# Sums of weight tiles in the SwiGLU pairs: from GpSimd to VectorE, with two low parts formed by ScalarE and an accumulating DMA, and the DRAM sums of the last weights issued earlier

## The chip, the cores and the metric

The kernel runs on one core of one Trainium2 chip. The metric is the time of one execution on the device in microseconds (us). The kernel before the change took 811.02 us (median of three runs: 810.82, 811.02 and 812.86).

Five engines work side by side, and the text uses the profile's names for them: PE multiplies matrices (PEld is its loading of weights), DVE (VectorE) and POOL (GpSimd) work on whole tiles, ACT (ScalarE) does activations and casts, and SP (SyncE) only issues transfers here. Each runs its own list of instructions in order and waits on semaphores for the others. Transfers (DMA) are issued by SP or by POOL and carried out by 16 DMA engines.

## What is computed

One decoder block on x of shape 512 x 1024 in float32, cut to what matters:

```python
h = rmsnorm(x, norm1_g)
z_glu, z_rx, z_rg, z_ga, z_gb = split(h @ w_in + b_in)   # the input stage
y_a = convolution mixer of z_glu, then @ conv_w_out + conv_b_out
y_b = (linear recurrence of z_rx, times gelu(z_rg)) @ lru_w_out
x = x + (sigmoid(z_ga) * y_a + sigmoid(z_gb) * y_b) @ w_mix_out
h = rmsnorm(x, norm2_g)
x = x + (silu(h @ ffn_w1) * (h @ ffn_w3)) @ ffn_w2       # SwiGLU, D_FF = 2816
return rmsnorm(x, norm_f_g)
```

## The kernel before, in words

**Products.** A product in float32 is made of three faster ones: each operand is kept as a high part (its value rounded) and a low part (what the rounding left), and PE multiplies high by high, high by low and low by high. Every weight tile is loaded by SP into a raw buffer of 128 x 1024 (512 KB; tag `raw`, 8 buffers). ACT casts it to the high part (`split_to`, line 124), and DVE or POOL subtracts high from raw to make the low part (`sub`, line 120; the argument `lo` says which engine). Both parts lie in one buffer of tag `hl` (5 of them). The tiles stand in one list, `chunks`. `weights(key)` asks for a tile and brings everything up to four tiles further (`AHEAD`) into the program at the same place; `emit_chunk` writes the load, the cast and the subtraction of one tile, and calls what the list has under `after`.

**Stages.** The input stage goes through a table of 60 tokens (`ORDER`); each makes one or two tiles of z (24 matmuls a tile) or, in tokens `h`, gates of the recurrence. POOL makes the low parts of nearly all its weights. Then come eight steps with the weights of the recurrence's output (tiles `lo`), eight steps with those of the convolution's output (`co`), the product with `w_mix_out`, the SwiGLU, and the products with `ffn_w2` (line 1247, results `or`). In the first stages the order of PE, ACT, DVE and SP is the one written in the code; in the SwiGLU loop the framework's scheduler places the instructions of each engine, and keeps their dependencies.

**The SwiGLU pairs.** D_FF is taken in 11 pairs of 2 x 128 columns. Pair 0 is plain. Each of the pairs 1 to 10 multiplies the 2 x 2 blocks of h and of the weights by a scheme of seven products in place of eight (class `Seven`). The seven weight tiles of a pair are b11, b21, b22, t2, t1, t3 and t4; w1 and w3 lie side by side in the halves of a tile, and each product takes 24 matmuls of 256 columns (line 1441). t1 to t4 are sums and differences of b11, b12, b21 and b22. For pairs 1 to 3 they are made in the input stage by POOL and stored in DRAM (`make_f_sums`). For pairs 4 to 10 `f_fly(k)` makes them where they are used: SP loads the four tiles (line 382, two transfers of 256 KB each, one for w1 and one for w3), and POOL makes four sums in the raw buffers themselves (`in_line`): b12 + b22 goes over b12 and is t3, that plus b11 goes over b11 and is t2, b22 minus t2 goes over b22 and is t1, b21 plus t2 goes over b21 and is t4. All seven low parts of such a pair are made by DVE.

Beside these, DVE adds and subtracts the results out of PSUM (`c11`, `q`, `c12`, `c21`), ACT applies SiLU to one half of each (`out_of`, line 1458), and DVE multiplies the halves (line 1459, into `ou` and `ov`).

**The sums of the last weights.** The products with `ffn_w2` use the same scheme, and its sums t1 to t4 (tiles `ot1` to `ot4` in DRAM) are made by transfers alone: `out_sums` is a generator of 48 transfers from DRAM to DRAM, 24 plain copies (line 486) and 24 that add to what is there (line 487), nearly all of 512 KB, interleaved over six groups. POOL issues them. In the kernel before, `in_line` draws from this generator between POOL's sums (1, 3 and 3 in each pair); each is placed behind the newest sum.

Of the kernel before, what the change touches and what calls it, by code (L numbers as in the profile page):

```python
# [8 lines left out]
F32 = mybir.dt.float32  # L9
F32R = mybir.dt.float32r  # L10
AF = mybir.ActivationFunctionType
ALU = mybir.AluOpType

P = 128
# [38 lines left out]
BEGUN, BEGUN_LATER = (1, 2), (3,)  # L53
STORED = BEGUN + BEGUN_LATER
OUT_SUMS_OF = 2
SUMS_AT, SUMS_STEP, SUMS_LAG, STORE_LAG = 3, 5, 2, 2
STORED_LAG = 3
SUMS_OWN = 40
# [26 lines left out]
def tile_block(ctx, tc, a, out):  # L85
# [24 lines left out]
    vec, act, pe, pool_e = nc.vector, nc.scalar, nc.tensor, nc.gpsimd  # L110


    add = lambda o, x, y: vec.tensor_tensor(out=o, in0=x, in1=y, op=ALU.add)  # L113
    plus_on = lambda eng, o, x, y: eng.tensor_tensor(out=o, in0=x, in1=y, op=ALU.add)  # L114

    newest = {}
    put_off = []

    def sub(eng, o, x, y):
        return eng.tensor_tensor(out=o, in0=x, in1=y, op=ALU.subtract)  # L120

    def split_to(h, l, full, eng, copy=act.copy):

        copy(h, full)  # L124
        if eng is None:
            put_off.append((l, full, h.bitcast(F32)))
            return h, l
        last = sub(eng, l, full, h.bitcast(F32))
        newest["sub" if eng is pool_e else "low"] = last.ins
        return h, l  # L130
# [26 lines left out]
    def wchunk(key, src, kt, cols, where="hl", lo=pool_e, after=None):  # L157
        chunks.append((key, src, kt, cols, where, lo, after))
# [191 lines left out]
    def f_quarter(n, k, w_, c0, c1):  # L350

        c, j = 4 * (int(n[1]) - 1), 2 * k + int(n[2]) - 1
        return w_[:, c + c0 : c + c1, j * P : (j + 1) * P]
# [20 lines left out]
    def f_fly(k):  # L374

        q = {}

        def new(n):
            q[n] = raw_t = raws.tile([P, 1024], F32, tag="raw", name=f"raw_f{n}_{k}")
            for i, w_ in enumerate((w1, w3)):  # L380
                src = f_quarter(n, k, w_, 0, 4)
                newest["any"] = nc.sync.dma_start(raw_t[:, i * T : (i + 1) * T].rearrange("p (k n) -> p k n", k=4), src).ins
            return raw_t

        def in_line(n, make, *what):
            with tc.issue_after(newest["sum"]) if "sum" in newest else nullcontext():
                newest["sum"] = make(pool_e, *what).ins
            for _ in range(n):
                next(out_steps, None)

        def first():
            raw_t = new("b11")
            new("b12")
            return raw_t

        def sums_32():
            in_line(0, plus_on, q["b12"], q["b22"], q["b12"])
            in_line(1, plus_on, q["b11"], q["b12"], q["b11"])

        def sums_14():  # L400
            in_line(3, sub, q["b22"], q["b11"], q["b22"])
            in_line(3, plus_on, q["b21"], q["b21"], q["b11"])

        for n, load, after in (
            ("b11", first, None), ("b21", lambda: new("b21"), None), ("b22", lambda: new("b22"), sums_32),
            ("t2", lambda: q["b11"], sums_14), ("t1", lambda: q["b22"], None), ("t3", lambda: q["b12"], None), ("t4", lambda: q["b21"], None),
        ):
            wchunk(f"f{n}_{k}", None, 8, P, where=load, lo=vec, after=after)

    def f_chunks(k, some=("b2", "t0", "t1")):  # L410

# [78 lines left out]
    def out_sums():  # L490

        rows = outq.w.rearrange("p (k i) n -> p i k n", i=2)
        jobs = []
        for k0 in range(0, KF, OUT_SUMS_OF):
            ks = slice(k0, min(k0 + OUT_SUMS_OF, KF))
            jobs.append(dram_sums(lambda i, h: rows[:, i, ks, h * T : (h + 1) * T], {n: v[:, ks, :] for n, v in outq.all_sums.items()}))
        for start, dst, src in (one for of in zip(*jobs) for one in of):
            with tc.issue_after(newest["sum"]):
                start(dst, src)
            yield  # L500

# [441 lines left out]
    def run_beside(n):  # L943
        for _ in range(n):
            if not beside_one():
                break
            room[0] -= 1
# [203 lines left out]
    f_todo = [f_piece(k, i, c) for k in STORED for i in range(2) for c in range(2)]  # L1151
    f_sums_steps = make_f_sums()
    out_steps = out_sums()
    with tc.manual_schedule(engines={ET.PE, ET.Activation, ET.DVE, ET.SP}):
        for kind, j in ORDER:
            next(f_sums_steps, None)
            if kind == "u" and j < EARLY:
                for _ in glu(j, in_mm(GLU + j), in_mm(GLU + 8 + j)):
                    pass
                run_beside(2)  # L1160
                emit_to(emitted[0] + 2)
                continue
            if kind == "u":
                pv = step(GLU, j)
                end_step()
                later(glu(j, pv, step(GLU + 8, j)), 1)
            elif kind == "rx":
                later(rx(j, step(RX, j)), 1)
            elif kind == "rg":
                later(rg(j, step(RG, j)), 1)  # L1170
            elif kind == "gb":
                later(half_sig(j, step(GB, j)), 1)
            elif kind == "ga":
                later(sig(GA, j, step(GA, j), sga, "sga"), 1)
            elif kind == "h":
                later(heads(j, head_mms(j)))
                continue
            end_step()
        while held_back:
            at_step[0] += 1  # L1180
            run_due()


    for j in range(8):
        ws = w_tiles(f"lo{j}_0", 5) + w_tiles(f"lo{j}_1", 5)
        ps = bank(f"yb{j}")
        mm3(ps, ws, y)
        vec.scalar_tensor_tensor(out=sgb[j], in0=sgb[j], scalar=1.0, in1=ps, op0=ALU.add, op1=ALU.mult)
        run_beside(7)
        next(f_sums_steps, None)  # L1190
        if j in (2, 4, 6):
            mixq.make_sums(j // 2 - 1)
    yb = sgb
# [116 lines left out]
    for n, j in enumerate(mixq.order()):  # L1310
        ws = w_tiles(f"co{j}", ND)
        ps = bank(f"ya{j}")
        mm3(ps, ws, un)
        o = sga[j]
        vec.scalar_tensor_tensor(out=o, in0=ps, scalar=pc("conv_b_out", j), in1=o, op0=ALU.add, op1=ALU.mult)
        m7.tile(j, lambda cs, dst: add(dst, o[:, cs], yb[j][:, cs]))
        if n == 0:
            mixq.make_sums(3)
        if n == 5:
            x2 = [[longt(f"x2{t}{h}") for h in range(2)] for t in range(NT)]  # L1320
            for t in range(NT):
                for h in range(2):
                    nc.sync.dma_start(x2[t][h], x_nat[:, t, h * T : (h + 1) * T])
        next(f_sums_steps, None)

    for _ in f_sums_steps:
        pass


# [131 lines left out]
    class Seven:  # L1461
# [14 lines left out]
        def copy(self):  # L1476
            self.c11 = shortt(f"c11_{self.k}")
            left_over(act.copy(self.c11, self.r1).ins)
# [242 lines left out]
```

## Time and profile before

| | us |
|---|---|
| median of three runs | 811.02 |
| the profiled execution | 811.09 |
| its span, first to last instruction | 809.3 |
| PE busy in the span | 787.3 (97%), 4327 instructions |
| DVE | 712.1 (88%), 958 instructions |
| ACT | 471.5 (58%), 697 instructions |
| POOL | 366.3 (45%), 259 instructions |
| the chain that ended last, by engine | PE 78%, DVE 15%, DMA 3% |
| memory traffic | 132.14 MB read, 35.65 MB written, 207 GB/s over the span |

The figures come from one execution taken by the hardware profiler. An engine is called busy while one of its instructions runs; register and semaphore instructions and the issuing of DMAs don't count. The chain that ended last is followed back from the last instruction, at each step to what released it. The granted clock is the share of full speed at which PE was allowed to run. A share of DMA time is the time that packets took against that of 16 engines, and can read over 1 where packets overlap. Shares over the whole span are means over stages with different limits; so the views below are taken by stage.

### The profile page before, as it was taken

How to read it: one execution, taken by the hardware profiler on the slowest of the kernel's cores; microseconds unless marked ns; L12 is line 12 of the kernel's file. 1: busy time of each engine (PE TensorE's matmuls, PEld its weight loads, DVE VectorE, ACT ScalarE, POOL GpSimd, SP SyncE). 2: the span in 40 equal slices, each digit the busy share in tenths (PEclk: the TensorE clock that was granted, in tenths of full speed). 3: DMA queues.
4: the chain of work that ended last, by engine and by line, in shares of the span. 5: the costliest groups of instructions: out<-in, count | busy, mean ns of one | idle time of the engine just before them, and what ended most of it. 6: DMA issues, size and time to landing. Idle time of an engine off the chain costs nothing.

```text
span 809.3 us, 12207 instructions
## 1 busy us (share of the span) xinstructions
PE 787.3 (97%) x4327; PEld 687.8 (85%) x4327; DVE 712.1 (88%) x958; ACT 471.5 (58%) x697; POOL 366.3 (45%) x259
## 2 busy tenths in 40 slices
PE   9999999999999999999999999999898989999996
PEld 8888888888888888888888989999898979988885
DVE  6489998998988985899978687799999999999956
ACT  8444769976775876473336675544343433756744
POOL 4366756766856456537101520177555766000000
PEclk9999999999999999999999999999898999999999
DMA  7828996897595334765686454669999898969622
GB/s 239 225 57 236 233 257 179 238 241 201 162 254 163 111 121 140 237 197 157 218 236 199 140 183 133 181 164 201 265 216 264 155 273 175 298 219 304 201 65 104
DMA packets 180334, 158.64 MB, mean 196 GB/s; under 512 B 14106, under 2 KB 144818, under 8 KB 180274
## 3 DMA queue, kind: packets, MB, share of 16 engines
q1 hardware_dynamic: 170322, 132.43, 56.1%
q0 software_dynamic: 9792, 25.17, 13.6%
q8 instruction: 34, 0.56, 0.3%
q10 hardware_dynamic: 160, 0.27, 0.1%
q14 instruction: 26, 0.21, 0.1%
HBM read 132.14 MB, written 35.65 MB: 207 GB/s over the span
## 4 chain that ended last, share of the span: by engine, by line
PE 78%; DVE 15%; DMA 3%; issue 2%; SPq 0%; POOL 0%; ACT 0%; DVEq 0%; ACTq 0%
PE z L621 35%; PE or L1247 13%; PE fr L1441 7%; PE yb L621 7%; PE ya L621 5%; PE mxr L1247 5%; DVE ov L1459 5%; DVE hl_ft L120 4%; PE f L621 3%; DVE hl_fb L120 2%; PE g L1074 2%; DMA raw_fb<-in_ffn_w_dram 2%; DVE c L113 1%; PE fr L1495 1%; DVE q L120 1%
## 5 line engine op out<-in xcount | busy, mean ns | idle before, releaser
L874 DVE SCALAR_TENSOR_TENSOR cv<-u,par,cv 128x507 f32<-128x507 f32 (+15 forms) x240 | 162.2, 732 | 4.2 <-ACT cv L870 3.3
L120 POOL TENSOR_TENSOR hl_in<-raw_in,hl_in 128x1024 fp32r<-128x1024 f32 (+1 forms) x52 | 122.7, 2370 | 94.5 <-ACT hl_in L124 87.6
L114 POOL TENSOR_TENSOR raw_fb<-raw_fb,raw_fb 128x1024 f32<-128x1024 f32 x21 | 63.5, 3026 | 86.9 <-DMA raw_fb<-in_ffn_w_dram 45.5
L1441 PE MATMUL fr<-hs_0h,hl_ft 128*128 128x256 f32 x320 | 66.3, 304 | 13.6 <-DVE hl_ft L120 13.6
L1441 PEld LDWEIGHTS fr<-hs_0h,hl_ft 128*128 128x128 f32 x320 | 55.7, 211 | 14.8 <-DVE hl_ft L120 14.8
L1458 ACT ACTIVATE c<-c 128x256 f32<-128x256 f32 x30 | 12.2, 416 | 74.6 <-DVE c L113 74.6
L120 DVE TENSOR_TENSOR hl_fb<-raw_fb,hl_fb 128x1024 fp32r<-128x1024 f32 x29 | 50.6, 1747 | 3.2 <-ACT hl_fb L124 3.2
L120 DVE TENSOR_TENSOR hl_ft<-raw_fb,hl_ft 128x1024 fp32r<-128x1024 f32 x28 | 52.8, 1887 | 0.0
L124 ACT CAST hl_in<-raw_in 128x1024 fp32r<-128x1024 f32 x50 | 51.4, 1047 | 2.0 <-DMA th<-tg 0.8
L1441 PE MATMUL fr<-hs_0l,hl_ft 128*128 128x256 f32 x160 | 48.0, 300 | 0.0
L120 POOL TENSOR_TENSOR hl_ot<-raw_ot,hl_ot 128x1024 fp32r<-128x1024 f32 x1 | 2.4, 2400 | 100.6 <-ACT hl_ot L124 100.6
L621 PE MATMUL z<-h10h,hl_in 128*128 128x512 f32 (+1 forms) x108 | 41.1, 382 | 0.0
L621 PE MATMUL z<-h12h,hl_in 128*128 128x512 f32 (+1 forms) x108 | 40.8, 379 | 0.0
L621 PE MATMUL z<-h13h,hl_in 128*128 128x512 f32 (+1 forms) x108 | 40.8, 379 | 0.0
L621 PE MATMUL z<-h14h,hl_in 128*128 128x512 f32 (+1 forms) x108 | 40.8, 379 | 0.0
L621 PE MATMUL z<-h15h,hl_in 128*128 128x512 f32 (+1 forms) x108 | 40.8, 379 | 0.0
L621 PE MATMUL z<-h16h,hl_in 128*128 128x512 f32 (+1 forms) x108 | 40.8, 379 | 0.0
L621 PE MATMUL z<-h11h,hl_in 128*128 128x512 f32 (+1 forms) x108 | 40.8, 379 | 0.0
L621 PE MATMUL z<-h17h,hl_in 128*128 128x512 f32 (+1 forms) x108 | 40.8, 379 | 0.0
L120 POOL TENSOR_TENSOR hl_lo<-raw_lo,hl_lo 128x640 fp32r<-128x640 f32 x16 | 26.6, 1668 | 27.6 <-ACT hl_lo L124 27.6
L124 ACT CAST hl_fb<-raw_fb 128x1024 fp32r<-128x1024 f32 x30 | 31.0, 1043 | 13.4 <-PE fr L1441 7.6
L114 POOL TENSOR_TENSOR fws<-fws 128x256 f32<-128x256 f32 x48 | 36.5, 761 | 2.7
(950 smaller groups left out, 2703.4 us busy)
## 6 DMA issues: line engine op xcount, KB each, us to landing
raw_in<-in_w_in_dram SPq DMA_DIRECT2D x51, 512.0 KB
raw_fb<-in_ffn_w_dram SPq DMA_DIRECT2D x74, 256.0 KB
ot<-in_ffn_w_dram POOLq DMA_DIRECT2D x30, 512.0 KB, 7.7
raw_ob<-in_ffn_w_dram SPq DMA_DIRECT2D x33, 256.0 KB
raw_ot<-ot SPq DMA_DIRECT2D x33, 256.0 KB
fws<-in_ffn_w_dram SPq DMA_DIRECT2D x12, 512.0 KB
raw_lo<-in_lru_w_out_dram SPq DMA_DIRECT2D x16, 320.0 KB
ot<-ot POOLq DMA_DIRECT2D x10, 512.0 KB, 6.8
```

Of the source, the lines that this page charges most:

```text
L113: add = lambda o, x, y: vec.tensor_tensor(out=o, in0=x, in1=y, op=ALU.add)
L114: plus_on = lambda eng, o, x, y: eng.tensor_tensor(out=o, in0=x, in1=y, op=ALU.add)
L120: return eng.tensor_tensor(out=o, in0=x, in1=y, op=ALU.subtract)
L124: copy(h, full)
L621: pe.matmul(ps, l, r, start=i == 0, stop=i == n - 1)
L874: vec.scalar_tensor_tensor(out=acc[:, s:], in0=u[c][:, : T - s], scalar=dw(c, s), in1=acc[:, s:], op0=ALU.mult, op1=ALU.add)
L1074: pe.matmul(ps[:HB], head_chunk[0][:ROWS_G, g, h % 2, m, :], ext[h][m][:ROWS_G], start=m == 0, stop=m == 1)
L1247: pe.matmul(banks[i][:, cs], l_[:, ts], r_[:, cs], start=start and n == 0, stop=stop and n == 2, skip_group_check=again)
L1441: pe.matmul(ps[:, HALVES[i]], lw[:, c, :], rx_, start=not (again or i or c or m), stop=bool(i and c == 3 and m == 2), skip_group_check=True,)
L1458: act.activation(c[:, LO], c[:, LO], AF.Silu)
L1459: newest["now"] = vec.tensor_tensor(out=dst, in0=c[:, LO], in1=c[:, HI], op=ALU.mult).ins
L1495: pe.matmul(self.r4[:, HALVES[i]], lw, rx_, start=not (i or c or m), stop=bool(i and c == 3 and m == 2), skip_group_check=True)
```

## The change

It does three things.

1. `in_line` goes. In pairs 4 to 10 the four sums of a pair are made by DVE (`add` and `sub(vec, ...)`), in the same buffers.
2. Two of the seven low parts of such a pair, those of b21 and of t3 (`LOWS_BY_DMA`), are no longer subtracted by DVE. ACT casts the high part as before, then writes the negated raw tile, rounded in the same way, to the place of the low part (new line 127), and POOL issues a DMA from the raw tile to that place that adds to what is there (new line 128); raw minus rounded is left there.
3. The 48 transfers of `out_sums` are issued earlier: one at every second token of the input stage, one with each of the eight `lo` steps, one with each of the eight `co` steps, and what is left behind the last of these. Each is placed behind the newest low part that POOL made, in place of the newest sum.

```diff
--- before.py
+++ after.py
@@ -53,6 +53,7 @@
 BEGUN, BEGUN_LATER = (1, 2), (3,)
 STORED = BEGUN + BEGUN_LATER
 OUT_SUMS_OF = 2
+LOWS_BY_DMA = ("b21", "t3")
 SUMS_AT, SUMS_STEP, SUMS_LAG, STORE_LAG = 3, 5, 2, 2
 STORED_LAG = 3
 SUMS_OWN = 40
@@ -122,6 +123,10 @@
     def split_to(h, l, full, eng, copy=act.copy):
 
         copy(h, full)
+        if eng == "dma":
+            act.activation(l, full, AF.Copy, scale=-1.0)
+            pool_e.dma_start(l.bitcast(F32), full, accum_op=ALU.add)
+            return h, l
         if eng is None:
             put_off.append((l, full, h.bitcast(F32)))
             return h, l
@@ -382,30 +387,24 @@
                 newest["any"] = nc.sync.dma_start(raw_t[:, i * T : (i + 1) * T].rearrange("p (k n) -> p k n", k=4), src).ins
             return raw_t
 
-        def in_line(n, make, *what):
-            with tc.issue_after(newest["sum"]) if "sum" in newest else nullcontext():
-                newest["sum"] = make(pool_e, *what).ins
-            for _ in range(n):
-                next(out_steps, None)
-
         def first():
             raw_t = new("b11")
             new("b12")
             return raw_t
 
         def sums_32():
-            in_line(0, plus_on, q["b12"], q["b22"], q["b12"])
-            in_line(1, plus_on, q["b11"], q["b12"], q["b11"])
+            add(q["b12"], q["b22"], q["b12"])
+            add(q["b11"], q["b12"], q["b11"])
 
         def sums_14():
-            in_line(3, sub, q["b22"], q["b11"], q["b22"])
-            in_line(3, plus_on, q["b21"], q["b21"], q["b11"])
+            sub(vec, q["b22"], q["b11"], q["b22"])
+            add(q["b21"], q["b21"], q["b11"])
 
         for n, load, after in (
             ("b11", first, None), ("b21", lambda: new("b21"), None), ("b22", lambda: new("b22"), sums_32),
             ("t2", lambda: q["b11"], sums_14), ("t1", lambda: q["b22"], None), ("t3", lambda: q["b12"], None), ("t4", lambda: q["b21"], None),
         ):
-            wchunk(f"f{n}_{k}", None, 8, P, where=load, lo=vec, after=after)
+            wchunk(f"f{n}_{k}", None, 8, P, where=load, lo="dma" if n in LOWS_BY_DMA else vec, after=after)
 
     def f_chunks(k, some=("b2", "t0", "t1")):
 
@@ -495,7 +494,7 @@
             ks = slice(k0, min(k0 + OUT_SUMS_OF, KF))
             jobs.append(dram_sums(lambda i, h: rows[:, i, ks, h * T : (h + 1) * T], {n: v[:, ks, :] for n, v in outq.all_sums.items()}))
         for start, dst, src in (one for of in zip(*jobs) for one in of):
-            with tc.issue_after(newest["sum"]):
+            with tc.issue_after(newest["sub"]):
                 start(dst, src)
             yield
 
@@ -1151,9 +1150,13 @@
     f_todo = [f_piece(k, i, c) for k in STORED for i in range(2) for c in range(2)]
     f_sums_steps = make_f_sums()
     out_steps = out_sums()
+    at_out = [0]
     with tc.manual_schedule(engines={ET.PE, ET.Activation, ET.DVE, ET.SP}):
         for kind, j in ORDER:
             next(f_sums_steps, None)
+            at_out[0] += 1
+            if at_out[0] % 2 == 0:
+                next(out_steps, None)
             if kind == "u" and j < EARLY:
                 for _ in glu(j, in_mm(GLU + j), in_mm(GLU + 8 + j)):
                     pass
@@ -1188,6 +1191,7 @@
         vec.scalar_tensor_tensor(out=sgb[j], in0=sgb[j], scalar=1.0, in1=ps, op0=ALU.add, op1=ALU.mult)
         run_beside(7)
         next(f_sums_steps, None)
+        next(out_steps, None)
         if j in (2, 4, 6):
             mixq.make_sums(j // 2 - 1)
     yb = sgb
@@ -1322,8 +1326,11 @@
                 for h in range(2):
                     nc.sync.dma_start(x2[t][h], x_nat[:, t, h * T : (h + 1) * T])
         next(f_sums_steps, None)
+        next(out_steps, None)
 
     for _ in f_sums_steps:
+        pass
+    for _ in out_steps:
         pass
```

What this does to the engines' lists is shown below. A row has the line in the code, the operation, output <- inputs, and the shape. Names of raw tiles are `raw_f`, the block and the pair (`raw_fb12_6` is the buffer of b12 of pair 6); the last number is a running one. Line numbers after the change are higher by 1 to 7.

**DVE, in the pairs.** First the list before, from the tail of pair 6 into the low parts of pair 7:

```order
L120 TENSOR_TENSOR hl_fb21_7_5947<-raw_fb21_7_5944,hl_fb21_7_5947 128x1024
L120 TENSOR_TENSOR q_6_5940<-fr5_6_5878,q_6_5940 128x512
L113 TENSOR_TENSOR c12_6_5975<-fr3_6_5877,q_6_5940 128x512
L120 TENSOR_TENSOR hl_fb22_7_5982<-raw_fb22_7_5979,hl_fb22_7_5982 128x1024
L1459 TENSOR_TENSOR ou6_5814<-c12_6_5975 128x256
L120 TENSOR_TENSOR q_6_5940<-q_6_5940,fr7_6_5879 128x512
L120 TENSOR_TENSOR hl_ft2_7_6017<-raw_fb11_7_5907,hl_ft2_7_6017 128x1024
L1459 TENSOR_TENSOR ov6_5815<-q_6_5940 128x256
L113 TENSOR_TENSOR c21_6_6012<-fr1_6_5816,c21_6_6012 128x512
```

The same place after the change, one pair earlier (tail of pair 5, low parts of pair 6):

```order
L114 TENSOR_TENSOR raw_fb12_7_5943<-raw_fb22_7_6013,raw_fb12_7_5943 128x1024
L121 TENSOR_TENSOR q_5_5739<-fr5_5_5677,q_5_5739 128x512
L114 TENSOR_TENSOR c12_5_5775<-fr3_5_5676,q_5_5739 128x512
L121 TENSOR_TENSOR hl_fb22_6_5782<-raw_fb22_6_5779,hl_fb22_6_5782 128x1024
L1466 TENSOR_TENSOR ou5_5612<-c12_5_5775 128x256
L121 TENSOR_TENSOR raw_fb22_6_5779<-raw_fb11_6_5706,raw_fb22_6_5779 128x1024
L121 TENSOR_TENSOR q_5_5739<-q_5_5739,fr7_5_5678 128x512
L121 TENSOR_TENSOR hl_ft2_6_5816<-raw_fb11_6_5706,hl_ft2_6_5816 128x1024
L1466 TENSOR_TENSOR ov5_5613<-q_5_5739 128x256
L114 TENSOR_TENSOR raw_fb21_6_5743<-raw_fb21_6_5743,raw_fb11_6_5706 128x1024
L114 TENSOR_TENSOR c21_5_5811<-fr1_5_5614,c21_5_5811 128x512
```

The low part of b21 has left the list. Three sums have come in: that of b12 and b22 of pair 7 stands at the head of these eleven rows, two pairs ahead of the results around it (pair 5), and those over b22 and b21 of pair 6 stand between low parts and results.

**ACT, in the pairs,** after the change, from the SiLU of pair 5's last result (`c21_5`) into the low part of t3 of pair 6:

```order
L125 CAST hl_ft1_6_5850<-raw_fb22_6_5779 128x1024
L1485 COPY c11_6_5877<-fr1_6_5848 128x512
L1465 ACTIVATE c21_5_5811<-c21_5_5811 128x256
L125 CAST hl_ft3_6_5881<-raw_fb12_6_5709 128x1024
L127 ACTIVATE hl_ft3_6_5881<-raw_fb12_6_5709 128x1024
L125 CAST hl_ft4_6_5913<-raw_fb21_6_5743 128x1024
```

New is the row of line 127: it stands behind the SiLU of `c21_5` in ACT's list, and the accumulating DMA of t3 of pair 6 follows it.

**SP, in the pairs.** The load of the four raw tiles of pair 7, with the semaphores that each row waits for (DMAHW and DMASW are those of transfers issued by SP and by POOL). Before:

```order
L382 DMA raw_fb12_7_5910<-in_ffn_w1_dram 128x4x128 [waits DMAHW4_49,Pool_49]
L382 DMA raw_fb12_7_5910<-in_ffn_w3_dram 128x4x128 [waits DMAHW5_49]
L382 DMA raw_fb21_7_5944<-in_ffn_w1_dram 128x4x128 [waits DMAHW6_49,DVE_49]
L382 DMA raw_fb21_7_5944<-in_ffn_w3_dram 128x4x128 [waits DMAHW7_49]
L382 DMA raw_fb22_7_5979<-in_ffn_w1_dram 128x4x128 [waits DMAHW0_49,DVE_49]
L382 DMA raw_fb22_7_5979<-in_ffn_w3_dram 128x4x128 [waits DMAHW1_49]
```

After:

```order
L387 DMA raw_fb12_7_5943<-in_ffn_w1_dram 128x4x128 [waits DMAHW4_49,DVE_49]
L387 DMA raw_fb12_7_5943<-in_ffn_w3_dram 128x4x128 [waits DMAHW5_49]
L387 DMA raw_fb21_7_5977<-in_ffn_w1_dram 128x4x128 [waits DMAHW6_49,DVE_49]
L387 DMA raw_fb21_7_5977<-in_ffn_w3_dram 128x4x128 [waits DMAHW7_49]
L387 DMA raw_fb22_7_6013<-in_ffn_w1_dram 128x4x128 [waits DMAHW0_49,DMASW7_49]
L387 DMA raw_fb22_7_6013<-in_ffn_w3_dram 128x4x128 [waits DMAHW1_49]
```

There are eight raw buffers and a pair takes four of them, so a load takes over a buffer of two pairs before. The load of b22 of pair 7 takes the one that held b12 of pair 5, and t3 of pair 5 after the sum; it now waits for the transfer DMASW7, the accumulating DMA that makes the low part of that t3, in place of a DVE instruction.

**POOL, at the end of the input stage.** Before:

```order
L120 TENSOR_TENSOR hl_in7_2130<-raw_in7_2007,hl_in7_2130 128x1024
L120 TENSOR_TENSOR hl_in15_2187<-raw_in15_2063,hl_in15_2187 128x1024
L120 TENSOR_TENSOR hl_in49_2250<-raw_in49_2114,hl_in49_2250 128x1024
L120 TENSOR_TENSOR hl_in30_2253<-raw_in30_2165,hl_in30_2253 128x1024
L120 TENSOR_TENSOR xb9l_2249<-xb9_2228,xb9h_2248 128x512
```

After:

```order
L121 TENSOR_TENSOR hl_in7_2148<-raw_in7_2024,hl_in7_2148 128x1024
L486 DMA ot3_86<-in_ffn_w2_dram 128x2x512
L121 TENSOR_TENSOR hl_in15_2206<-raw_in15_2081,hl_in15_2206 128x1024
L486 DMA ot3_86<-in_ffn_w2_dram 128x2x512
L121 TENSOR_TENSOR hl_in49_2270<-raw_in49_2132,hl_in49_2270 128x1024
L121 TENSOR_TENSOR hl_in30_2273<-raw_in30_2184,hl_in30_2273 128x1024
```

The copies stand between POOL's low parts of input weights. Of the 48 transfers 17 copies and 12 additions are issued in the input stage, 1 and 6 beside the `lo` steps, and 6 and 6 beside the `co` steps. In the SwiGLU pairs POOL's list then holds the 14 accumulating DMAs of line 128 and no other instruction.

## The prediction

> **What bounds the kernel now.** I read the busy times by stage first, then the chain that ended last, then single engines inside the stage that stands out. Columns of the first view: stretch, its length, busy time of PE, weight loads, DVE, ACT and POOL (with instruction counts), PE's granted clock, DMA share, GB/s.
>
> ```profile
> 70.00:200.00 130.00, 130.00 (x573) 105.52 (x573) 119.57 (x173) 97.06 (x132) 87.49 (x65) 1.00 0.85 228
> 200.00:310.00 110.00, 110.00 (x486) 90.37 (x486) 94.97 (x137) 81.04 (x102) 66.37 (x44) 1.00 0.57 161
> ...
> 499.20:529.50 30.30, 30.30 (x255) 30.30 (x254) 22.13 (x26) 14.64 (x21) 5.96 (x3) 1.00 0.55 160
> 554.00:578.60 24.60, 21.27 (x155) 21.07 (x154) 24.57 (x17) 9.89 (x16) 16.01 (x11) 0.86 1.01 226
> ```
>
> In the first three stretches PE never idles. In the SwiGLU pairs 4 to 10, of which the last row shows a part, it does (21.27 of 24.60), its clock falls to 0.86, and DVE is full (24.57 of 24.60). So DVE bounds this stage, PE the others. How much there is to win say the first matmul of pair 4 (timeline) and two pieces of the chain that ended last (start, length, what):
>
> ```profile
> 533.52 0.28 PE L1441 MATMUL fr<-h20h,hl_fb 128*128 128x256 f32 x1
> ...
> 499.13 30.25 PE fr L1441 x252
> ...
> 698.09 103.39 PE or L1247 x456
> ```
>
> Pair 4 starts at 533.52 and the output products at 698.09: 164.6 us for 7 pairs. Without waits 252 matmuls take 30.25 us, 0.120 each; a pair is 7 products of 24, so 2.88 us a product and 20.16 a pair, and 7 pairs are 141.1. **The stage holds 23.5 us** of waits and slow clock that a DVE out of the way could give back, and no more.
>
> Why is DVE full? Timeline of one pair, DVE and then POOL (start, length, instruction):
>
> ```profile
> 573.48 3.40 DVE L120 TENSOR_TENSOR hl_fb<-raw_fb,hl_fb 128x1024 fp32r<-128x1024 f32 x1
> ...
> 579.25 0.42 DVE L1459 TENSOR_TENSOR ou<-c 128x256 f32<-128x256 f32 x1
> ...
> 582.94 5.22 DVE L1459 TENSOR_TENSOR ov<-q 128x256 f32<-128x256 f32 x1
> ...
> 593.48 1.21 DVE L120 TENSOR_TENSOR hl_ft<-raw_fb,hl_ft 128x1024 fp32r<-128x1024 f32 x1
> 594.62 0.68 DVE L113 TENSOR_TENSOR c<-fr,c 128x512 f32<-128x512 f32 x1
> 595.22 1.21 DVE L120 TENSOR_TENSOR hl_ft<-raw_fb,hl_ft 128x1024 fp32r<-128x1024 f32 x1
> ...
> 575.74 0.70 POOL L486 DMA_DIRECT2D ot<-in_ffn_w_dram  x1
> ...
> 586.15 3.54 POOL L487 DMA_DIRECT2D ot<-in_ffn_w_dram  x3
> ...
> 597.69 2.46 POOL L114 TENSOR_TENSOR raw_fb<-raw_fb,raw_fb 128x1024 f32<-128x1024 f32 x1 [5.56 <-issue]
> ```
>
> The same subtraction takes 1.21 us, or 3.40 where a POOL sum (2.4 to 2.5 us) lies beside its start; a 256-wide product takes 0.42 or 5.22. From start to start DVE needs 1.14 us for 1024 columns (593.48 to 594.62), 0.60 for 512 (594.62 to 595.22), and by the same slope about 0.33 for 256.
>
> **What the change costs, part by part.**
>
> *POOL's sums go*: 28 instructions (21 additions, 7 subtractions), and with them what stretches DVE. *DVE gets the four sums and loses two lows of each pair*: 5 lows and 4 sums of 1024 columns, 5 instructions of 512, 4 of 256: 9 x 1.14 + 5 x 0.60 + 4 x 0.33 = 14.6 us per pair, against 23.5 now (164.6 / 7). That is below PE's 20.16: DVE's work alone no longer bounds.
>
> *ACT* gets two negations per pair, priced as the cast of the same size:
>
> ```profile
> L124 ACT CAST hl_fb<-raw_fb 128x1024 fp32r<-128x1024 f32 x30 | 31.0, 1043 | 13.4 <-PE fr L1441 7.6 <-issue 3.1 <-PE mxr L1247 2.0
> ...
> L1458 ACT ACTIVATE q<-q 128x256 f32<-128x256 f32 x10 | 4.2, 416 | 5.9 <-DVE q L120 5.9
> ...
> L1478 ACT COPY c<-fr 128x512 f32<-128x512 f32 x10 | 5.8, 579 | 1.1 <-PE fr L1441 1.0
> ```
>
> 2 x 1.04 on top of some 10 busy us a pair (9.89 above): 12 of 20, hidden beside PE, except where a negation stands in a chain.
>
> *The new waits* form one. (1) The low of t3 is ready only when its accumulating DMA has landed. (2) That DMA reads the raw tile of b12; by the order shown above, SP's load of b22 two pairs later takes over this buffer and waits for the landing. (3) The first sum of that later pair waits for this load, and stands in DVE's queue ahead of ten others, the last of which, c21 of the pair under way, releases the SiLU that ACT runs just ahead of the next t3's cast and negation. So the chain closes on itself once per pair:
>
> - DVE from the first sum to c21: 5 of 1024, 4 of 512, 2 of 256 columns, 5.7 + 2.4 + 0.7 = 8.8 us; ACT's SiLU, cast and negation 0.4 + 1.0 + 1.0; handovers 0.2 (estimate): **11.4 us**.
> - S, a load of b22 from its release (two transfers, one for each weight matrix): by the rows below an issue and then the second transfer to its landing, 0.59 + 3.56 = **4.2 us**; 0.59 + 4.61 = 5.2 where it meets other transfers.
> - D, negation to landed low. The trace has no accumulating DMA into SBUF. Nearest rows: 512 KB accumulated in DRAM, 6.2 at the fastest, 8.4 median; 512 KB plain out of SBUF, 3.4.
>
> Chain that ended last, then two lines of the program:
>
> ```profile
> 622.17 0.59 SPq L382
> 622.81 3.56 DMA raw_fb<-in_ffn_w_dram
> ...
> 548.87 4.61 DMA raw_fb<-in_ffn_w_dram
> ...
> L487 POOL DMA_DIRECT2D ot<-in_ffn_w_dram x24: 825/1576/3034, 539.9 to 684.4; - x24
> ...
> DMA to landing us min/median/max: 6.2/8.4/13.7
> ...
> L442 POOL DMA_DIRECT2D fs<-fws x4: 769/782/977, 240.4 to 321.0; - x4
> ...
> DMA to landing us min/median/max: 3.4/3.4/3.5
> ```
>
> I take **D = 6.2**: the same operation and size, while the 8.4 comes from up to three such DMAs in line (586.15) with DMA at 1.01, which the change relieves. Ends: 3.4 and 9.0 (a little over the median).
>
> So the loop is L = 11.4 + D + S = 21.8 us, 1.6 more than PE's pair. It runs five times (t3 of pair 4 to t3 of pair 9; no pair's loads follow those of pair 10). The first low has slack: its negation ends 0.58 + 0.42 + 2 x 1.04 = 3.1 us after the pair's first product, and the low is needed four products later, 11.5: 11.5 - 3.1 - 6.2 = 2.2. Loss on the stage: 5 x 1.6 - 2.2 = 6.0 us. **Won in the pairs: 23.5 - 6.0 = 17.5 us.** The chain of b21's low is shorter: D, three products and ACT's 3.1, 17.9 us, below 20.16. Pairs 1 to 3 ahead (DVE 22.13 of 30.30) take the first two sums, 2 x 1.14, in idle DVE time.
>
> A page speaks to D. By the Trainium skill, DMA: Bandwidth & Descriptors, section Anatomy of one DMA, a DMA that GpSimd issues takes about 2.0 us plus its bytes over 436 GB/s, 3.2 us for 512 KB (an estimate from that page). By it L would be 18.8, the loop would not bind, and the pairs would win all 23.5. The plain 3.4 agrees with it; the accumulating 6.2 does not.
>
> *The 48 DRAM transfers* of the last weights move out of the pairs: 29 into the input stage (17 copies, 12 additions), 7 beside the LRU output products, 12 beside the convolution's. Their engine time, and what PE needs for one tile of input weights:
>
> ```profile
> q0 software_dynamic: 9792, 25.17, 13.6%
> ...
> 73.85 5.46 PE z L621 x24
> ```
>
> 13.6% of 809.3 us over 52 transfers (these and 4 others) is 2.1 us each. Between 70 and 200 us some 14 fall: 29 us in 130, on a share of 0.85, gives 1.08, or 10 us too much. It can drain from 200 us on (0.57). POOL has room for issues of 0.7 to 1.6 us: it is busy 87 of 130. Loads run four tiles of 5.46 us ahead of PE, 22 us, so I expect the backlog to stay hidden but for **1 us**; bounds 0 and 10 (all of it as PE waits).
>
> **Sum.** The profiled execution took 811.09 (span 809.3 and 1.8 around it), the median of the runs is 811.02: the same. 811.1 - 17.5 + 1.0 = **794.6**.
>
> **Rivals.**
>
> 1. *PE bounds the pairs* (D + S up to 9.3): for it the plain 3.4, and SBUF on both sides; against it 6.2 as the least of 24. 811.1 - 23.5 + 0 to 1.5 = 787.6 to 789.1. The page's 3.2 gives the same. Chance 0.20.
> 2. *Slower*: the same loop over b12's buffer at D = 9.0 and S = 5.2: L = 25.6, loss 5 x 5.4 + 0.6 = 27.8, so 811.1 - 23.5 + 27.8 + 1.0 = 816.4. It decides from D of about 8.1 with that S, where the loop costs what the stretched DVE did. The median of 8.4 speaks for it, the emptier queue against it. Chance 0.05.
> 3. *Something adds 7 to 9 us.* DVE's denser work holds back POOL's issue: against it, the 0.70 issue at 575.74 ran beside a subtraction; for it, L487's median issue of 1.58 beside 0.78 for L442. One subtraction's 1.14 in every D costs 6 x 1.14: 801.4. Or the overload of 10 us reaches PE: 803.6. Chance 0.13 together. By the Trainium skill, SBUF — State Buffer, section Who interferes with whom, VectorE can starve GpSimd's writing of descriptors, but the section infers that sums of two tiles do not; by that the first half of this rival falls.
> 4. *The change doesn't do what it says*, and DVE stays full: each pair would need 9 us of stretching, and POOL's two issues of 1.6 give 3.2. Chance 0.02, at about 811.
>
> **How the numbers follow.** Forecast 794.6 (D of 5.5 to 7.2: 790.4 to 801) 0.60; the rivals 0.20, 0.05, 0.13, 0.02. The range goes from 787.5, the whole room, to 804, past rival 3. Faster by over 0.3% (about what a measurement of this kernel can tell from none): 0.60 + 0.20 + 0.13, less 0.02 for the tails, 0.91; same 0.03; slower 0.06.
>
> **What would show it.** Right: pairs 4 to 6 start 20.2 us apart, the later ones about 21.8; DVE's lows take 1.21 throughout; DVE idles before the sum of b12 and b22 until a load of raw_fb ends; what PE waits for is t3's low. Right of the input stage: PE busy throughout up to 530 us, DMA near 1 from 70 to 200. Wrong: landings of the new DMAs outside 5.5 to 7.2; PE waiting for hl_in, ext or hl_mx tiles before 450 us; DVE rows of over 2 us in the pairs.

## The result, and the profile after

The kernel after the change took 807.89 us (median of 16 runs, 806.03 to 813.73) against 811.52 before in the same runs; the ratio is 0.9962, 95% interval 0.9945 to 0.9979. The forecast was 794.6. The profiled execution took 806.7: its span is 804.9, with 1.8 around it.

The stretches of the profile after, columns as in the prediction: three of the input and mixer stages, then pairs 4 to 10 one by one.

```profile
70.00:200.00 130.00, 130.00 (x574) 105.50 (x573) 121.80 (x173) 97.17 (x132) 100.22 (x81) 1.00 1.01 276
200.00:310.00 110.00, 110.00 (x487) 90.36 (x486) 96.21 (x137) 81.18 (x101) 73.66 (x55) 1.00 0.83 221
310.00:420.00 110.00, 108.56 (x479) 89.45 (x478) 91.79 (x116) 51.26 (x75) 60.75 (x44) 1.00 0.91 249
535.16:555.32 20.16, 20.16 (x170) 20.16 (x169) 14.40 (x18) 11.38 (x17) 1.72 (x2) 1.00 0.65 157
555.32:575.48 20.16, 20.16 (x170) 20.16 (x169) 12.70 (x16) 10.86 (x14) 1.72 (x2) 1.00 0.66 158
575.48:597.81 22.33, 20.41 (x171) 20.21 (x170) 13.78 (x18) 11.52 (x16) 1.72 (x2) 1.00 0.62 142
597.81:623.23 25.42, 21.75 (x170) 21.55 (x169) 15.13 (x19) 11.50 (x16) 1.72 (x2) 0.93 0.55 125
623.23:646.23 23.00, 20.42 (x170) 20.21 (x169) 14.69 (x18) 11.51 (x16) 1.72 (x2) 1.00 0.61 136
646.23:673.50 27.27, 22.15 (x170) 21.74 (x169) 21.18 (x29) 14.61 (x22) 1.72 (x2) 0.94 0.45 118
673.50:693.66 20.16, 20.16 (x170) 20.16 (x169) 15.37 (x24) 12.04 (x17) 0.86 (x1) 1.00 0.67 186
```

DVE is no longer full (12.7 to 15.1 us in the first five pairs), and two pairs run at PE's 20.16 us. Then the pairs take 22.3, 25.4, 23.0 and 27.3 us, and the last 20.2 again. The stage lasts 158.5 us (535.16 to 693.66) where it lasted 164.6: 6.1 us won, not 17.5. It also starts 1.6 us later than before (533.52).

What PE waits for from 310 to 700 us, after (what waited, for what: us in all, times, longest):

```profile
PE fr L1448 <- DMA hl_ft<-raw_fb: 12.5, 4, 4.3
PE ya L620 <- POOL hl_co L121: 1.4, 1, 1.4
PE fr L1448 <- ACT c L1485: 0.8, 1, 0.8
```

In the pairs it is the low part of t3, made by the accumulating DMA, for 12.5 of 13.3 us. The 1.4 us outside them is one wait for the low part of a weight tile of the convolution's output (at 372 us).

Two rounds of the loop that the prediction described, after (timeline; start, length, instruction). First the round from t3 of pair 4, up to the sum that waits for the load:

```profile
541.65 0.86 POOL L128 DMA_DIRECT2D hl_ft<-raw_fb  x1 [11.41 <-ACT hl_ft L127]
547.81 0.92 SPq L387 DMA_DIRECT2D raw_fb<-in_ffn_w_dram  x2
549.97 0.86 POOL L128 DMA_DIRECT2D hl_fb<-raw_fb  x1 [7.46 <-DMA raw_fb<-in_ffn_w_dram]
551.76 1.23 DVE L114 TENSOR_TENSOR raw_fb<-raw_fb,raw_fb 128x1024 f32<-128x1024 f32 x1 [3.52 <-DMA raw_fb<-in_ffn_w_dram]
```

Then the fifth round, from t3 of pair 8 to t3 of pair 9:

```profile
634.61 0.86 POOL L128 DMA_DIRECT2D hl_ft<-raw_fb  x1 [19.13 <-ACT hl_ft L127]
639.19 0.86 POOL L128 DMA_DIRECT2D hl_fb<-raw_fb  x1 [3.71 <-DVE raw_fb L114]
640.59 1.70 SPq L387 DMA_DIRECT2D raw_fb<-in_ffn_w_dram  x2
648.17 1.23 DVE L114 TENSOR_TENSOR raw_fb<-raw_fb,raw_fb 128x1024 f32<-128x1024 f32 x1 [8.93 <-issue]
...
656.44 0.69 DVE L114 TENSOR_TENSOR c<-fr,c 128x512 f32<-128x512 f32 x1
657.16 0.42 ACT L1465 ACTIVATE c<-c 128x256 f32<-128x256 f32 x1 [1.37 <-DVE c L114]
658.43 1.05 ACT L127 ACTIVATE hl_ft<-raw_fb 128x1024 fp32r<-128x1024 f32 x1
659.78 0.86 POOL L128 DMA_DIRECT2D hl_ft<-raw_fb  x1 [19.73 <-ACT hl_ft L127]
```

The loop is there link by link: t3's DMA, b22's load as soon as it lands, DVE's sum behind the load, c21, its SiLU, the negation, the next t3's DMA. The view gives no landing for a load. By the semaphore updates in the trace the sum starts 0.08 us after the last piece of b22's load has landed in all five rounds (at 648.09 in the fifth, whose row says `issue`). The five rounds, read in the same way; the last column says when the DMA for b21's low is issued, against the load of b22:

| round | D, DMA to landing | S, landing to sum | sum to next DMA | period | b21's DMA against the load |
|---|---|---|---|---|---|
| forecast | 6.2 | 4.2 | 11.4 | 21.8 | none given |
| 1 | 6.15 | 3.96 | 11.61 | 21.72 | 2.2 behind |
| 2 | 6.15 | 4.83 | 11.60 | 22.58 | 0.6 behind |
| 3 | 6.21 | 6.29 | 11.61 | 24.11 | 1.6 ahead |
| 4 | 6.18 | 6.78 | 11.60 | 24.56 | 1.6 ahead |
| 5 | 5.96 | 7.60 | 11.61 | 25.17 | 1.4 ahead |

D and the work of the engines came out as forecast. S grew from 4.0 to 7.6, and b21's DMA went from behind the load to ahead of it. The loop brings that about itself: from round 1 to round 2 b21's DMA comes 20.16 us later, at PE's pace, and the load 21.72 later, at the loop's.

### The profile page after: what moved, and what is told of

Its sections match the earlier page's. It is cut to its first block, busy times and chain, and to the rows that moved or that the text cites. A ratio compares the mean times of both kernels' runs of the same rounds, so it can differ in the third digit from the quotient of the medians.

```text
span 804.9 us, 12214 instructions
## 1 busy us (share of the span) xinstructions
PE 782.3 (97%) x4327; PEld 682.9 (85%) x4327; DVE 653.3 (81%) x972; ACT 484.5 (60%) x711; POOL 306.0 (38%) x245
## 4 chain that ended last, share of the span: by engine, by line
PE 83%; DMA 5%; issue 5%; DVE 4%; POOL 1%; ACT 1%; SPq 0%; DVEq 0%; POOLq 0%; ACTq 0%
PE z L620 35%; PE fr L1448 19%; PE or L1251 13%; PE mxr L1251 5%; PE ya L620 5%; DMA hl_ft<-raw_fb 3%; PE f L620 3%; PE g L1073 2%; DVE mxws L114 1%; PE fr L1502 1%; DMA mxt<-mxws 1%; DMA mxws<-in_w_mix_out_dram 1%; DVE u L920 1%; DMA x<-in_x_dram 1%; PE th L665 0%
## 5 line engine op out<-in xcount | busy, mean ns | idle before, releaser
L1448 PE MATMUL fr<-hs_0h,hl_ft 128*128 128x256 f32 x320 | 59.3, 283 | 0.8 <-ACT c L1485 0.8
L114 DVE TENSOR_TENSOR raw_fb<-raw_fb,raw_fb 128x1024 f32<-128x1024 f32 x21 | 25.6, 1223 | 36.5 <-DMA raw_fb<-in_ffn_w_dram 26.9
L1448 PEld LDWEIGHTS fr<-hs_0h,hl_ft 128*128 128x128 f32 x320 | 50.6, 192 | 1.0 <-ACT c L1485 1.0
L128 POOL DMA_DIRECT2D hl_ft<-raw_fb x7 | 6.0, 864 | 111.0 <-ACT hl_ft L127 111.0
L1448 PE MATMUL fr<-hs_1h,hl_ft 128*128 128x256 f32 x160 | 33.7, 302 | 12.5 <-DMA hl_ft<-raw_fb 12.5
L1448 PE MATMUL fr<-hs_0l,hl_ft 128*128 128x256 f32 x160 | 45.3, 283 | 0.0
L115 POOL TENSOR_TENSOR fws<-fws 128x256 f32<-128x256 f32 x48 | 38.5, 802 | 5.2 <-DMA fws<-in_ffn_w_dram 3.2
L1448 PEld LDWEIGHTS fr<-hs_1h,hl_ft 128*128 128x128 f32 x160 | 28.0, 209 | 13.3 <-DMA hl_ft<-raw_fb 13.3
L128 POOL DMA_DIRECT2D hl_fb<-raw_fb x7 | 6.0, 862 | 86.1 <-ACT hl_fb L127 57.9
```

What stands on the lines that cost most here:

```text
L128: pool_e.dma_start(l.bitcast(F32), full, accum_op=ALU.add)
L1448: pe.matmul(ps[:, HALVES[i]], lw[:, c, :], rx_, start=not (again or i or c or m), stop=bool(i and c == 3 and m == 2), skip_group_check=True,)
```

## The experiments

Two questions: is it the loop that holds the pairs, and what makes S long; and which of the three parts of the change won what it won. The results, each against the kernel before in the same runs:

| label | kernel | median us | ratio, 95% interval |
|---|---|---|---|
| e4_sum_late | change, first two sums later in DVE's order | 790.00 | 0.9726 (0.9710 to 0.9742) |
| e8_b22_first | change, b22 loaded ahead of b21 | 791.19 | 0.9737 (0.9715 to 0.9758) |
| e1_b21_only | change, t3's low on DVE | 792.82 | 0.9751 (0.9731 to 0.9770) |
| e3_none | change, both lows on DVE | 789.57 | 0.9733 (0.9702 to 0.9764) |
| e2_t3_only | change, b21's low on DVE | 800.56 | 0.9842 (0.9819 to 0.9864) |
| e12_b21_thin | change, b21's DMA cut to 32 columns | 800.76 | 0.9871 (0.9835 to 0.9907) |
| e5_pool_sums | before, DRAM transfers moved | 788.94 | 0.9720 (0.9706 to 0.9735) |
| e9_thin | e5 with 48 thin transfers in the pairs | 813.37 | 1.0026 (1.0012 to 1.0041) |
| e11_full | e5 with 48 whole transfers in the pairs | 813.73 | 1.0031 (1.0016 to 1.0046) |
| e10_dve_sums | before, sums on DVE | 855.12 | 1.0534 (1.0517 to 1.0552) |
| e7_in_pairs | change, DRAM transfers left in the pairs | 878.91 | 1.0834 (1.0799 to 1.0869) |
| e6_rest_later | e3, 19 transfers later | 802.41 | 0.9884 (0.9870 to 0.9899) |

### Opening the loop

The expectations call two answers theory A (the time is lost in the loop, and any way of opening it gives the time back) and theory C (the transfers hold the pairs back whatever the order).

**e4_sum_late** keeps all work and both DMAs, and changes only where two sums stand in DVE's list.

```diff
         def sums_32():
-            add(q["b12"], q["b22"], q["b12"])
-            add(q["b11"], q["b12"], q["b11"])
+            with tc.issue_after(newest["now"]):
+                add(q["b12"], q["b22"], q["b12"])
+                add(q["b11"], q["b12"], q["b11"])
```

> As after the change, with both lows by DMA, but the first two sums of a pair are kept in VectorE's order behind the newest product of the SwiGLU results (one pair ahead instead of two). Theory A: the sum that waits for the load of b22 no longer stands ahead of c21, the loop is open, PE bounds the pairs, 789 to 792, though the DMAs take as long as before (D 6.1, S 4 to 7.6). Theory C (transfers hold back the pairs whatever the order of VectorE): 799 to 808.

790.00. Two of its pairs, and the DMAs of line 128 by their time to landing:

```profile
536.52:556.68 20.16, 20.16 (x171) 20.16 (x170) 15.17 (x20) 11.82 (x17) 1.71 (x2) 1.00 0.67 158
637.32:657.48 20.16, 20.16 (x171) 20.16 (x170) 15.13 (x22) 12.58 (x17) 1.72 (x2) 1.00 0.60 157
...
DMA to landing us min/median/max: 4.5/6.0/7.3
```

PE runs at 20.16 us a pair though the DMAs take up to 7.3 us, longer than after the change. So neither the DMAs nor DVE's amount of work held the pairs; the order of DVE's list did, which put the waiting sum ahead of c21.

**e8_b22_first** opens the same loop at another link: the raw tile of b22 is loaded ahead of b21's, so that b21's load takes over t3's buffer, and DVE's order is left as it was.

```diff
             new("b12")
+            new("b22")
             return raw_t
...
-            ("b11", first, None), ("b21", lambda: new("b21"), None), ("b22", lambda: new("b22"), sums_32),
+            ("b11", first, None), ("b21", lambda: new("b21"), None), ("b22", lambda: q["b22"], sums_32),
```

> The change with one line moved: the raw tile of b22 is loaded ahead of that of b21, so that b21's load and not b22's takes over the buffer of t3 of two pairs before and waits for its accumulating DMA. VectorE's order keeps the sum of b12 and b22 ahead of c21, and both lows are made by DMA. Theory A: the loop is open at this link, 789 to 792. Theory C (order of VectorE or the DMAs themselves): 799 to 808.

791.19, and no wait of PE in pairs 4 to 10. **e1_b21_only** (`LOWS_BY_DMA = ("b21",)`) takes the DMA out of the loop:

> Only b21's low is formed by ScalarE and the accumulating DMA; t3's low is subtracted by VectorE again (DVE 15.7 us a pair). Theory A (the time is lost in the loop from t3's accumulating DMA over the load of b22 to the first sum and back to t3's negation): the load of b22 now waits for a subtraction, D leaves the loop, the loop is 11.7 us + S (4 to 7.6) = 16 to 19, below 20.16, and PE bounds the pairs: 811.1 - 23.5 + 1.6 = 789 to 792. Theory C (accumulating DMAs, their issue or the fuller DMA engines hold back the pairs whatever the loop): half of the DMAs stay, so 796 to 802.

792.82 (790.02 to 793.1), 0.8 above the range of theory A and 3 below that of theory C. The profiled execution took 790.02, and PE waits for nothing in its pairs; what the slower executions lost is not known. **e3_none** (`LOWS_BY_DMA = ()`) has no accumulating DMA in the pairs at all:

> No low by DMA: VectorE makes all seven lows and the four sums of a pair, 16.9 us of work. Theory A: no accumulating DMA in any chain, PE bounds the pairs, 789 to 792. Rival (DVE at 16.9 us plus the wait of the first sum for the load of b22, S above 7, bounds): 793 to 800.

789.57: all seven lows and the four sums fit beside PE. In this kernel part 2 of the change relieves an engine that had no need of it, and costs 18.3 us (807.89 less 789.57). Four kernels that open the loop in four ways end within 3.3 us of each other, and in their profiles PE has no wait in pairs 4 to 10.

### What makes S long

**e2_t3_only** (`LOWS_BY_DMA = ("t3",)`):

> Only t3's low is formed by ScalarE and the accumulating DMA; b21's low is subtracted by VectorE, and stands inside the loop, which gets 1.14 us longer on DVE. Theory A with S made long by b21's accumulating DMA that is issued about 1.5 us before the load of b22: without it S is 4.0 in every pair, D 5.5 to 6.2, the period of t3's DMAs 22.2 to 22.9 throughout, total 798 to 801. Rival B (S is long because all raw loads of a pair come in one burst, b21's DMA or not): S grows to 6 or 7.6 as after the change, periods 24 to 26, total 806 to 813.

800.56, in the range of theory A. In the four rounds in which the sum waited for the load, S was 3.88, 4.54, 3.89 and 5.10 and not 7.6. But D was 5.1 to 7.1 there, the periods 21.6 to 24.8 where 22.2 to 22.9 were expected, and DVE's list is another, so the terms moved together. **e12_b21_thin** keeps every list and alters one size; it leaves out the addition for 992 of b21's 1024 columns:

```diff
-        if eng == "dma":
+        if eng in ("dma", "thin"):
...
-            pool_e.dma_start(l.bitcast(F32), full, accum_op=ALU.add)
+            c = slice(0, 32 if eng == "thin" else None)
+            pool_e.dma_start(l.bitcast(F32)[:, c], full[:, c], accum_op=ALU.add)
...
-            wchunk(f"f{n}_{k}", None, 8, P, where=load, lo="dma" if n in LOWS_BY_DMA else vec, after=after)
+            wchunk(f"f{n}_{k}", None, 8, P, where=load, lo={"b21": "thin", "t3": "dma"}.get(n, vec), after=after)
```

> The change, with one size altered: the accumulating DMA of b21's low adds only 32 of its 1024 columns (the other 992 columns of that low part are left as the negated raw values). All engines keep their lists, the loop stays closed. If b21's DMA ahead of the load of b22 is what lengthens S from 4.0 to 7.6 us: S 4.0 to 4.8 in all five rounds, periods 21.7 to 22.5, total 811.1 - 23.5 + 1.5 + 5 x (1.6 to 2.2) - 2 = 795 to 799. If S grows because the raw loads of a pair come in one burst: S still to 6 and more, 803 to 808.

S was 3.97, 5.28, 3.90, 3.94 and 5.18 (mean 4.5, against 5.9 after the change), the periods 20.9 to 23.1, the median 800.76, a little over the 795 to 799. The timeline of its third round, where the small DMA goes out 2.2 us ahead of the load (S is 3.90; after the change the third round has the whole DMA 1.6 us ahead, and 6.29):

```profile
589.87 0.85 POOL L129 DMA_DIRECT2D hl_fb<-raw_fb  x1 [3.72 <-DVE raw_fb L114]
592.03 0.92 SPq L388 DMA_DIRECT2D raw_fb<-in_ffn_w_dram  x2
595.91 1.23 DVE L114 TENSOR_TENSOR raw_fb<-raw_fb,raw_fb 128x1024 f32<-128x1024 f32 x1 [5.99 <-DMA raw_fb<-in_ffn_w_dram]
```

The trace after the change shows the same from the other side. In its fifth round, from 641.5 to 644.5 us, while the load of b22 is under way, the DMA engines work almost for POOL's queue alone (packets, MB, share of the 16 engines; q0 has POOL's transfers, q1 SP's):

```profile
q0 software_dynamic: 120, 0.49, 106.2%
q1 hardware_dynamic: 117, 0.05, 7.3%
```

So most of the growth of S is the engine time of b21's accumulating DMA, 512 KB that go out ahead of the load of b22. Two rounds at 5.2 remain, the second and the fifth. In both, and in the second and fifth after the change, a packet of 16 KB of the queue that the profile calls `instruction` ran for 0.9 to 1.1 us in the middle of the load; in the other rounds of the two kernels no packet of that size did. No run shows it to be the cause.

### Which part of the change won

**e5_pool_sums** leaves sums and lows where they were before and only issues the DRAM transfers where the change issues them (`in_line` as before, without its draws from `out_steps`).

> Only the third part of the change: the sums of pairs 4 to 10 stay on POOL and all lows on VectorE, the 48 DRAM transfers are issued where the change issues them. If POOL's sums alone stretch VectorE's instructions (as the prediction had it), the pairs stay near 23.5 us each: 810 to 813. If the issues of the transfers and their DMAs did part of it: four sums of 2.43 us stretch 12.3 us of VectorE work to some 21.5, 797 to 804. If the transfers did all of it: 789 to 791.

788.94: this third part alone wins more than the whole change. But not for the reason that the matching line of the expectation gives, since POOL's sums still stretch DVE. DVE's groups from 536 to 676 us, before and then e5 (busy us, mean ns of one):

```profile
L120 DVE TENSOR_TENSOR hl_fb<-raw_fb,hl_fb 128x1024 fp32r<-128x1024 f32 x18 | 35.1, 1948 | 0.0
L1459 DVE TENSOR_TENSOR ov<-q 128x256 f32<-128x256 f32 x6 | 33.5, 5579 | 0.0
```

```profile
L121 DVE TENSOR_TENSOR hl_fb<-raw_fb,hl_fb 128x1024 fp32r<-128x1024 f32 x18 | 30.0, 1665 | 2.6 <-DMA raw_fb<-in_ffn_w_dram 1.5 <-ACT hl_fb L125 1.0
L1470 DVE TENSOR_TENSOR ov<-q 128x256 f32<-128x256 f32 x7 | 13.9, 1988 | 0.0
```

The product that took 5.6 us takes 2.0, where it needs 0.42. DVE is nearly full and just fits under PE, as a pair of e5 shows:

```profile
554.90:575.06 20.16, 20.16 (x170) 20.16 (x169) 19.59 (x17) 10.12 (x15) 10.92 (x5) 1.00 0.37 106
```

Of the transfers, is it the bytes or POOL's issuing that holds DVE? **e9_thin** and **e11_full** put 48 spare transfers back between POOL's sums, 16 columns wide or 512:

```diff
+        w_ = 16
+        dup = {n: dram.tile([P, KF, w_], F32, tag=f"du{n}", name=f"du{n}") for n in ("t1", "t2", "t3", "t4")}
...
+            for _ in range(n):
+                next(dup_steps, None)
```

In e11_full `w_` is 512; `n` is 0, 1, 3 and 3 behind the four sums of a pair.

> As the run that moves the DRAM transfers alone (788.9), and besides 48 transfers between POOL's sums in pairs 4 to 10, placed as before the change, of as many rows but 16 elements of each row in place of 512 (1/32 of the bytes; they go to a spare place in DRAM that nothing reads). If it was POOL's issuing of transfers beside its sums that held VectorE's instructions (3.1 us each in the trace of before, 1.8 with sums alone): pairs of 22 to 23.5 us, 802 to 813. If it was the bytes moved: 789 to 791.

> As the thin run, with whole rows of 512 elements: the 48 extra transfers have the size of those before the change. It must give back the pairs of before, 23.5 us each: 810 to 815. If thin and full agree, bytes don't matter; if thin is near 789 and full near 811, they are the cause.

813.37 and 813.73: the same, and both within 0.3% of the time before. The thin kernel's profile, the stretch that was shown of before, and the 256-wide product (its line is 1487 there):

```profile
554.00:578.60 24.60, 21.28 (x165) 21.08 (x165) 24.57 (x17) 9.92 (x14) 16.33 (x12) 0.93 0.41 91
```

```profile
L1487 DVE TENSOR_TENSOR ov<-q 128x256 f32<-128x256 f32 x6 | 33.5, 5586 | 0.0
```

DVE is busy 24.57 of 24.60 as before, at a DMA share of 0.41 instead of 1.01. So it isn't the bytes: that POOL issues the transfers between its sums is enough. (The thin ones have as many rows as the whole ones; what part of the issuing does it is open.) **e10_dve_sums** is the other half: sums on DVE, transfers in the pairs (a copy of 8 columns on POOL keeps their place).

```diff
+            newest["sub"] = pool_e.tensor_copy(mark, q[of][:, :8]).ins
+            for _ in range(n):
+                next(out_steps, None)
```

Here `n` is 1, 3 and 3 behind the sums over b11, b22 and b21.

> Only the first part of the change: the four sums of a pair on VectorE, all seven lows on VectorE, the 48 DRAM transfers in pairs 4 to 10 as before (a copy of 8 columns on POOL ahead of each group keeps their place). If the transfers hold VectorE only together with POOL's sums: VectorE needs 16.9 us a pair, PE bounds, and the 1.4 us at 372 us are saved, 787.5 to 789.5. If the fuller DMA engines delay the load of b22 by so much that the first sum stalls VectorE (12.9 + S over 20.16 from S = 7.3): 790 to 815.

855.12, far over the expectation. What DVE waits for, and then PE, from 536 to 720 us:

```profile
DVE raw_fb L114 <- DMA raw_fb<-in_ffn_w_dram: 80.3, 5, 17.4
```

```profile
PE fr L1451 <- DVE hl_fb L121: 49.8, 5, 11.9
```

The holds are gone, but the first sum now waits up to 17.4 us for its load behind transfers that POOL, free of sums, issues in bursts, and DVE stands still with it. Before, POOL came to that sum 6 to 9 us after the load had landed, by the trace's semaphore updates. **e7_in_pairs** adds the lows by DMA to that (issues behind the accumulating DMAs of line 128):

> Sums on VectorE and both lows by DMA as in the change, but the 48 DRAM transfers stay in pairs 4 to 10, in POOL's list behind the accumulating DMAs. The loop then has D and S under a DMA share of about 1 (before: S about 7 in such pairs, a DMA behind others on POOL's queue 8.4 to 13.7): L = 11.6 + 8.4 + 7 = 27 and more, 811.1 - 23.5 + 5 x 7 = 822 to 850, slower than before. If the loop's length doesn't follow the queue: 806 to 810.

878.91. The same sum, from 520 to 740 us:

```profile
DVE raw_fb L114 <- issue: 72.7, 4, 19.7
DVE raw_fb L114 <- DMA raw_fb<-in_ffn_w_dram: 27.2, 2, 25.6
```

In all five rounds this sum starts 0.07 to 0.08 us after the last piece of b22's load has landed, also where the row says `issue`. S is 15.3 to 22.7 us and D 6.2 to 9.5: the direction was forecast, the size not, and again S is the term that was too small. DVE's groups show no hold although 62 issues stand on POOL in the pairs of this kernel:

```profile
L121 DVE TENSOR_TENSOR hl_fb<-raw_fb,hl_fb 128x1024 fp32r<-128x1024 f32 x12 | 14.6, 1217 | 1.6 <-ACT hl_fb L125 1.6
```

**e6_rest_later** takes e3 and leaves 19 of the transfers out of the `lo` and `co` steps:

> No low by DMA, and the 19 transfers that the change issues beside the lo and co steps are left to POOL after the w_mix_out product. If the 1.4 us that PE waits at 372 us for the low part of a co tile come from those transfers, this wait is gone: 787.5 to 788.5, 1.4 below the same kernel with them (789.6). If they come from the 29 transfers of the input stage, no difference: 789 to 790. If the transfers then collide with pairs 1 to 5: above 791.

802.41. PE's wait at 372 us is gone, so it came from the transfers beside the `lo` steps (the first of the `co` steps is issued only at 373.45). But with nothing on POOL to pace them the 19 go out in one stretch, between 466 and 500 us, and PE loses 7.4 of 35 us ahead of pair 4, at a DMA share of 1.00:

```profile
310.00:420.00 110.00, 110.00 (x486) 91.03 (x485) 97.83 (x122) 52.86 (x77) 46.24 (x27) 1.00 0.67 206
499.00:534.00 35.00, 27.63 (x224) 26.82 (x223) 13.91 (x18) 12.23 (x16) 1.81 (x2) 0.97 1.00 244
```

The best of these kernels is e5_pool_sums, 788.9 us; its interval overlaps with those of e3_none, e4_sum_late and e8_b22_first. So part 3 alone brings the gain; part 1 on top of it (e3) adds nothing, alone it costs 44 us (e10), and part 2 gives most of the gain back.

## Why the prediction was wrong, point by point

- **The bound and the room** (23.5 us held by a full DVE in pairs 4 to 10): right. Five kernels with the loop open or absent run the pairs at or near 20.16 us, and e5's profiled execution, 788.97, is 811.1 - 23.5 and 1.4 us.
- **DVE's new work, 14.6 us a pair, and ACT hidden at 12**: right; 12.7 to 15.1 and 10.9 to 11.5 busy in the first five pairs, and no row of a sum or low over 1.23 us.
- **"with them what stretches DVE"** (POOL's sums): half right. Without them nothing is stretched. But beside sums alone an instruction is held 1.8 us on average, and DVE still fits under PE (e5); sums together with POOL's issues made the 23.5 (e9). The prediction saw the third part only as a cost of 1 us. It was the part that sufficed.
- **The loop**: its place, its five rounds and its closing over c21's SiLU are right, and shown by e4, e8 and e1. D = 6.2 was right (5.96 to 6.21), but partly by luck: it was the fastest of another kind, DRAM to DRAM, and the same DMA out of SBUF lands in 4.5 us at the least and in 6 and more beside loads. DVE and ACT took 11.6 against 11.4 (no row stood behind the 0.2 for handovers; from the negation's end to its DMA alone it is 0.3, 659.48 to 659.78); the slack was 1.8 (549.56, five products into pair 4, less 547.80) against 2.2. The 3.2 us worked out from the Trainium skill, DMA: Bandwidth & Descriptors, section Anatomy of one DMA, was reached by none of the accumulating DMAs of that size.
- **S = 4.2, at most 5.2**: the step that failed. Measured: 4.0 to 7.6, mean 5.9. It was taken from rows of before, without the transfer that the change itself puts ahead of this very load; b21's accumulating DMA made most of the growth (e12). And the two rows don't show whole loads. The chain infers what released an instruction of DVE; by the semaphore updates of that trace the load issued at 622.17 had landed at 627.92, and the five loads of b22 between 548 and 657 us took 5.8 to 7.0 us. With these the prediction's own sum gives 802.6 to 808.6. That this reaches the measured time would have been luck in part, for those loads ran beside the DRAM transfers that the change moves away.
- **The loss in the pairs, 6.0**: 17.4. The sum of the periods is 118.1, less 5 x 20.16 and 1.8: 15.5 us lost in the loop. Of the other 1.9, 1.7 is a clock of 0.50 for 3.4 us behind the last wait.
- **The moved transfers, 1 us in the input stage**: 1.6, nearly right in size, wrong in place. The input stage hid a DMA share of 1.01 as expected; the 1.4 us come from those beside the `lo` steps.
- **The sum** with the measured terms: 811.1 - 23.5 + 17.4 + 1.6 = 806.6, and the profiled execution took 806.7. This only says that the difference lies in these two places, for 17.4 is the stage's own 158.5 less 141.1.
- **Rivals and range**: rival 2 was the right loop with the wrong long term (D = 9.0 instead of S). Rival 3 did not occur: the issues of line 128 took 0.86 us or a little over throughout, and of the overload 1.4 us reached PE. The range ended at 804 because the end that was kept for S was itself too low; 7.6 in every round gives L = 25.2, a loss of 5 x 5.0 - 2.2 = 23 and 811.6.

## What to carry to other kernels

Before an engine is given less work, see what else ends with the change: here one of three parts brought the whole gain, and another gave most of it back. A transfer that makes an operand also keeps its source buffer until it lands; follow who takes over that buffer, and what stands in the queue behind the one who waits for it. If that closes a loop, move an instruction or a load in its queue rather than shorten its terms. When such a loop has a load in it, price the load beside the transfers that the change adds, not beside those of before.

## What the runs showed of the hardware

- **A VectorE operation with both inputs in SBUF is held while GpSimd adds tiles, and longer where GpSimd also issues DMAs.** By the traces, instructions held in pairs 4 to 10 took on average 1.8 us too long beside sums alone (25 of them in e5) and 3.1 beside sums and issues (22 before, 22 in e9 with 1/32 of the bytes). Beside issues alone none was held (e7). The Trainium skill, SBUF — State Buffer, section Who interferes with whom, has the first of these (two SBUF inputs contend with a GpSimd instruction that reads SBUF). Why issues lengthen the holds is open.
- **An accumulating DMA of 512 KB from SBUF to SBUF** took 4.5 us to land at the least and up to 7.3 beside loads (e4); one of 32 columns took 2.0 at the least (e12).
- **A load that SP issues is held up by a transfer that GpSimd issued 1.4 to 1.6 us earlier**: S of 6.3 to 7.6 us against 4.0. For 3 us of the fifth round the engines carried 0.49 MB of GpSimd's transfer and 0.05 MB of the load. The Trainium skill, DMA: Bandwidth & Descriptors, section Issuing engines are not separate DMA queues, states that transfers of both run on the same 16 DMA engines; the trace agrees.
